# A hybrid attention layer on one core: the compressed branch on four partition groups, and five events moved in the order of the work

## Chip, core and metric

The kernel runs on one core of a Trainium2 chip. The metric is the device time in microseconds (us). The kernel before took 374.5 us in the median of three runs (374.48 to 375.17). All data is float32; matmuls marked fp32r take their operands in the faster reduced form of float32.

## What is computed

One decoder layer for 256 tokens of width 1024, cut to what matters here:

```python
h = rmsnorm(x, norm1_g)
proj = h @ w_in            # NSA q | NSA k, v (3 branches) | gates | MoBA q, k, v | merge gates
kc = compress(k_c, pe_k, w1_k, w2_k)   # 15 overlapping blocks of 32 tokens:
vc = compress(v_c, pe_v, w1_v, w2_v)   #   gelu(block @ w1) @ w2
y_A = g0 * attn(q, kc, vc) + g1 * attn(q_rot, k_s, v_s) + g2 * attn(q_rot, k_w, v_w)
y_B = attn(qm_rot, km_rot, vm)         # MoBA; 256 tokens are one block
x += (sig(gA) * (y_A @ w_up_nsa) + sig(gB) * (y_B @ w_up_moba)) @ w_out
x += relu(rmsnorm(x, norm2_g) @ w_ff1) ** 2 @ w_ff2
return rmsnorm(x, norm_f_g)
```

The NSA part has 8 query heads on 2 key groups, the MoBA part 8 heads; a head has 64 columns. The compressed branch is `attn(q, kc, vc)` with the two `compress` calls: 15 compressed keys for each of the 2 groups, so 30 columns.

## The kernel before, in words

**Large products.** Each large float32 product is made of three fp32r matmuls (`mm3`, line 237): high part by high part, high by low, low by high. For this each weight chunk (1 MB, 128 x 2048) is loaded, ScalarE (ACT) rounds it to a high part (`whi`, line 114), and VectorE (DVE) subtracts to get the low part (`wlo`, line 116). There are three buffers each for raw chunks, high and low parts.

**Slots.** The work is a row of slots, one for each of the 60 weight chunks c (`CHUNKS`, line 24; the last two share one): 0 and 1 keys and values `kva`, 2 and 3 `kvb`, 4 and 5 NSA queries `q`, 6 and 7 MoBA queries `qm`, 8 and 9 `km`, 10 and 11 `vm`, 12 to 19 the merge gates, 20 to 23 the two up-projections `upn` and `upm`, 24 to 27 `wout`, from 28 on the feed-forward layer. A slot is a list of matmuls (24 in the projections), and `run_slot` (line 220) issues them in order on TensorE (PE). Everything else is an event: `at(0.45, f, ...)` puts the call f ahead of the first matmul at or beyond 0.45 of the slot's list, and all that f issues goes in that order to the queue of each engine. Events with equal positions keep the order in which they were noted. So the positions are an order written out by hand, and each engine takes its instructions strictly in that order. `split_events` (line 272) places the high parts, low parts and the next load of chunk c + 2; `std_events` picks their positions.

**Compressed branch.** `cmp_gather` and `gather_evac` (slot 3) put the keys and values of the 15 blocks into `kE`, for l = 0 to 15 a tile of 128 rows (two tokens by 64) and 30 columns. `cmp_mlp1` (slot 4, line 381) multiplies with the first weights: 32 matmuls with 64 weight columns, keys into partitions 0 to 63, values into 64 to 127, 30 columns moving; behind it stands the GELU chain on ACT and DVE. `cmp_mlp2` (slot 5, line 393) applies the second weights and spreads the results into block-diagonal `bdk` (for the scores) and `bdv` (for the values). `cmp_scores` (slot 7, line 416) makes the scores of 8 heads in 8 matmuls, each with 128 query rows as weights and the 30 columns of `bdk` moving, and runs the softmax on the same tile. `cmp_probs_t` (slot 8, line 438) transposes the probabilities in 8 pieces of 30 columns into `pcT`. `d_trans` (line 518) later multiplies `bdv` and `pcT` into the output of each NSA head pair.

**Window, selected and MoBA attention.** Units d = 0 to 5 (`unit_events`, line 563) do two heads in two branches, or four MoBA heads, in the odd slots from 9: scores (`d_scores`), row maxima on DVE (`d_max`), eight exponentials on ACT (`d_exp`), then normalising, transposing and multiplying with the values (`d_pv`).

**PSUM banks.** The projections alternate between two banks (`acc0`, `acc1`; `tp` joins at the gates), and `tp` and `yb` serve the small work. A bank is free again when ACT or DVE has evicted it; `evac_tm` (line 296) evicts a projection's half.

**Feed-forward.** A round is one `ff1` chunk (48 matmuls of 256 columns) and one `ff2` chunk. The first 13 `ff2` chunks use seven products instead of eight (`seven_mms`, line 929), each into its own bank; the last of the seven, "4", is issued in two halves of 256 columns (`mm3_halves`, line 242) from the second round on, and whole in the first. `combine` (line 941) later adds the seven banks in three steps. `act_parts` makes the high and low parts (`ah`, `al`) of the activations.

Of the kernel before, what the change touches and what calls it, by code (L numbers as in the profile page):

```python
# [17 lines left out]
NCMP = 15  # L18
# [27 lines left out]
def hybrid_layer(ctx: ExitStack, tc: tile.TileContext, gxd, w, w1c, small, const, gf, out):  # L46
# [79 lines left out]
    pcT = ap_.tile([128, 4, 256], F32, name="pcT")  # L126
    bdv = ap_.tile([128, 128], F32, name="bdv")
# [27 lines left out]
    pool.memset(pcT, 0.0)  # L155
    pool.memset(bdv, 0.0)
# [85 lines left out]
    def mm3_halves(o, lh, ll, rh, rl, first, last):  # L242

        return [m for x in (slice(0, 256), slice(256, 512))
                for m in mm3(o[:, x], lh, ll, rh[:, x], rl[:, x], first, last)]
# [35 lines left out]
    def std_events(c):  # L281
        if 9 <= c < 20 and c % 2:
            split_events(c, (0.0, 0.06), (0.09, 0.46))
        elif 9 <= c < 20:
            split_events(c, (0.0, 0.45), (0.3, 0.8))
        else:
            split_events(c, (0.0, 0.45), (0.3, 0.46))
# [64 lines left out]
    kE = ap_.tile([128, 2, 16, 30], F32, name="kE")  # L352
    bdk = ap_.tile([128, 30], F32, name="bdk")
# [14 lines left out]
    def gather_evac(s):  # L368
        tp = U["kc", s]
        for l2 in range(2):  # L370
            p0 = l2 * 64
            v = tp[p0:p0 + 64].rearrange("p (g i l m) -> p g l i m", g=2, l=8, m=2)
            for lh in range(2):
                ls = slice(lh * 8, (lh + 1) * 8)
                o = kE[p0:p0 + 64, s, ls, :].rearrange("p l (g i) -> p g l i", g=2)
# [17 lines left out]
    def cmp_mlp2():  # L393
        tk = tp_tile()
        mm(tk[:, 0:30], w2[0:64, :], gl[0:64, 3, :], True, True)
        tv = tk[:, 128:256]
        mm(tv[0:30, 0:128], gl[64:128, 3, :], w2[64:128, :], True, True)
        dve.tensor_tensor(bdk, tk[:, 0:30], kc_[:, K_BDK:K_BDK + 30], op=ALU.mult)
        dve.tensor_tensor(bdv[0:30, :], tv[0:30, 0:128], kc_[0:30, K_BDV:K_BDV + 128],
                          op=ALU.mult)  # L400

    def gate_evac():
        for t in range(2):
# [8 lines left out]
    pcs = (ap_.tile([128, 256], F32, name="pcs")[:, 0:240]  # L412
           .rearrange("p (q t h i) -> p q t h i", q=4, t=2, h=2))
    st4 = ap_.tile([128, 112], F32, name="st4")[:, 0:64].rearrange("p (a b) -> p a b", a=4)

    def cmp_scores():
        tp = tp_tile()
        for p in range(4):
            for t in range(2):
                o = (p * 2 + t) * 30  # L420
                mm(tp[:, o:o + 30], qT[:, p, t * 128:(t + 1) * 128], bdk, True, True)
        s4 = tp[:, 0:240].rearrange("p (q t h i) -> p q t h i", q=4, t=2, h=2)
        for t in range(2):
            dve.tensor_tensor(pcs[:, :, t], s4[:, :, t],
                              cmpm[:, t, None, None, :].to_broadcast([128, 4, 2, NCMP]), op=ALU.add)
        s = pcs.rearrange("p q t h i -> p (q t h) i")
        dve.tensor_reduce(st4[:, 0], s, op=ALU.max, axis=AX)
        dve.tensor_scalar(st4[:, 0], st4[:, 0], -1.0e30, None, op0=ALU.max)
        dve.tensor_tensor(s, s, st4[:, 0, :, None].to_broadcast([128, 16, NCMP]), op=ALU.subtract)
# [4 lines left out]
        dve.tensor_tensor(st4[:, 3], st4[:, 2], gates[:, 0].rearrange("p q t h -> p (q t h)"),  # L434
                          op=ALU.mult)
        dve.tensor_tensor(s, s, st4[:, 3, :, None].to_broadcast([128, 16, NCMP]), op=ALU.mult)

    def cmp_probs_t():
        for i in range(2):
            tp = tp_tile()  # L440
            for j in range(2):
                for t in range(2):
                    o = j * 256 + t * 128
                    pe.transpose(tp[0:30, o:o + 128],
                                 pcs[:, 2 * i + j, t].rearrange("p h i -> p (h i)"), ident)
            act.activation(pcT[0:30, 2 * i:2 * i + 2, :].rearrange("p a q -> p (a q)"),
                           tp[0:30, :], AF.Copy)
# [70 lines left out]
    def d_trans(d):  # L518
# [19 lines left out]
        if kind == "n":  # L538
            mm(U["y"][:, p % 2], bdv, pcT[:, p, :], True, False)
# [45 lines left out]
    for sec, c0, n in groups:  # L585
# [6 lines left out]
        for i in range(2):  # L592
# [598 lines left out]
```

## Time and profile before

| | us |
|---|---|
| median of three runs | 374.5 |
| lowest and highest run | 374.48, 375.17 |
| the profiled execution | 373.52 |
| its span, first to last instruction | 371.5 |
| PE, DVE, ACT, POOL busy | 363.2, 310.2, 234.7, 4.9 |

The granted clock of TensorE is 0.995 of full speed on the mean. In the timeline and the chain a row gives the start in us from the span's first instruction, the duration, the engine, the line, the operation with output and inputs, the shape (for a matmul weight rows times weight columns, then moving elements), how many instructions the row merges, and in brackets the idle time before it with what ended it. PEld is the loading of weights, which overlaps PE. A matmul's duration contains its way through the pipeline, so the next one starts long before it ends. "SPq" and the like are an engine's queue, which issues DMAs. Helpers such as `mm` (line 235) carry the line for all their callers, so rows are told apart by their tiles.

### The profile page before, as it was taken

The page shows a single profiled execution, that of the slowest core. Times are in us where ns is not written, and L with a number is a line of the kernel's source. Part 1 is how long each engine was busy: PE and PEld are TensorE (multiplying, and loading weights), DVE is VectorE, ACT ScalarE, POOL GpSimd, SP SyncE. Part 2 cuts the span into 40 slices and gives each one's busy share as a digit, 9 for nine tenths or more (in the row PEclk, how much of TensorE's full clock was granted, in tenths as well). Part 3 has the DMA queues.
Part 4 walks back from the last instruction along what each step waited for, and adds up shares of the span by engine and source line. Part 5 has one row for each costly group of instructions (what it writes and reads, how often), then busy time and mean ns, then how long its engine had stood idle before and what let it go on. Part 6 is the DMA issues. An engine that isn't in the chain of part 4 may idle for free.

```text
span 371.5 us, 5941 instructions
## 1 busy us (share of the span) xinstructions
PE 363.2 (98%) x2387; PEld 321.2 (86%) x2387; DVE 310.2 (84%) x449; ACT 234.7 (63%) x352; POOL 4.9 (1%) x13
## 2 busy tenths in 40 slices
PE   8999999999999999999999999999999999999993
PEld 7998888877778887778999999999999999999973
DVE  4897677896868769766877999999999999995875
ACT  5983455847747567525465897876666677764522
POOL 1020000000000000000000000000000000000000
PEclk9999999999999999999999999999999999999997
DMA  8986535333444333532483655454555656654003
GB/s 281 392 326 226 196 109 213 113 115 114 141 160 153 114 114 130 211 128 100 168 313 124 248 226 205 168 192 181 182 215 220 226 228 227 225 178 165 0 0 113
DMA packets 11402, 66.28 MB, mean 178 GB/s; under 512 B 1264, under 2 KB 3056, under 8 KB 4080
## 3 DMA queue, kind: packets, MB, share of 16 engines
q1 hardware_dynamic: 10512, 64.55, 47.1%
q10 hardware_dynamic: 864, 1.38, 1.1%
q8 instruction: 18, 0.29, 0.3%
q14 instruction: 8, 0.07, 0.1%
HBM read 64.87 MB, written 1.05 MB: 177 GB/s over the span
## 4 chain that ended last, share of the span: by engine, by line
PE 88%; DVE 4%; ACT 3%; DMA 2%; issue 2%; POOLq 0%; POOL 0%; DVEq 0%; ACTq 0%
PE acc L235 58%; PE o L235 10%; PE yb L235 5%; PE tp L235 4%; PE qacc L235 3%; PE kvbacc L235 2%; DMA raw<-in_kva_dram 2%; DVE wlo L116 2%; PE Sa L531 1%; PE Sa L235 1%; ACT whi L114 1%; PE tp L321 1%; PE Sb L531 1%; DVE ust L491 1%; ACT P L501 1%
## 5 line engine op out<-in xcount | busy, mean ns | idle before, releaser
L116 DVE TENSOR_TENSOR wlo<-raw,whi 128x1024 fp32r<-128x1024 f32 (+3 forms) x85 | 109.8, 1311 | 14.0 <-ACT whi L114 14.0
L114 ACT ACTIVATE whi<-raw 128x1024 fp32r<-128x1024 f32 (+3 forms) x84 | 93.3, 1138 | 29.8 <-PE acc L235 22.0
L235 PE MATMUL acc<-h2h,whi 128*128 128x256 f32 x256 | 71.0, 277 | 0.0
L235 PE MATMUL acc<-h2l,whi 128*128 128x256 f32 x256 | 70.8, 277 | 0.0
L235 PE MATMUL acc<-h2h,wlo 128*128 128x256 f32 x256 | 70.8, 276 | 0.0
L235 PE MATMUL acc<-whi,hTh 128*128 128x512 f32 (+1 forms) x128 | 50.9, 398 | 0.3 <-ACT vm L301 0.3
L235 PE MATMUL acc<-wlo,hTh 128*128 128x512 f32 (+1 forms) x128 | 50.7, 396 | 0.2 <-DVE wlo L116 0.2
L235 PE MATMUL acc<-whi,hTl 128*128 128x512 f32 (+1 forms) x128 | 49.4, 386 | 0.0
L235 PEld LDWEIGHTS acc<-h2l,whi 128*128 128x128 f32 x256 | 48.1, 188 | 0.0
L235 PEld LDWEIGHTS acc<-h2h,whi 128*128 128x128 f32 x256 | 48.1, 188 | 0.0
L235 PEld LDWEIGHTS acc<-h2h,wlo 128*128 128x128 f32 x256 | 48.1, 188 | 0.0
L920 ACT ACTIVATE whi<-wt 128x2048 fp32r<-128x2048 f32 x13 | 25.0, 1922 | 25.7 <-PE acc L235 24.6
L922 DVE TENSOR_TENSOR wlo<-wt,whi 128x2048 fp32r<-128x2048 f32 x13 | 29.8, 2292 | 0.1
L235 PEld LDWEIGHTS acc<-whi,hTh 128*128 128x128 f32 x128 | 24.3, 190 | 6.4 <-issue 0.9
L235 PEld LDWEIGHTS acc<-wlo,hTh 128*128 128x128 f32 x128 | 24.2, 189 | 4.8 <-DVE wlo L116 0.9
L235 PEld LDWEIGHTS acc<-whi,hTl 128*128 128x128 f32 x128 | 24.2, 189 | 4.5
L913 DVE TENSOR_TENSOR sl<-raw,sh 128x1536 fp32r<-128x1536 f32 x13 | 22.9, 1758 | 0.0
L911 ACT ACTIVATE sh<-raw 128x1536 fp32r<-128x1536 f32 x13 | 19.4, 1490 | 2.9 <-PE acc L235 2.9
L235 PE MATMUL acc<-mxl,whi 128*128 128x256 f32 x64 | 17.8, 278 | 0.0
L235 PE MATMUL acc<-mxh,wlo 128*128 128x256 f32 x64 | 17.8, 278 | 0.0
L235 PE MATMUL acc<-mxh,whi 128*128 128x256 f32 x64 | 17.7, 276 | 0.0
L870 ACT ACTIVATE ah<-aq 128x896 fp32r<-128x896 f32 (+1 forms) x16 | 14.1, 880 | 3.9 <-PE acc L235 2.2
(270 smaller groups left out, 739.5 us busy)
## 6 DMA issues: line engine op xcount, KB each, us to landing
raw<-in_ff_dram SPq DMA_DIRECT2D x32, 1024.0 KB, 5.2
raw<-in_gm_dram SPq DMA_DIRECT2D x8, 1024.0 KB, 4.8
raw<-in_wout_dram SPq DMA_DIRECT2D x4, 1024.0 KB, 4.8
raw<-in_q_dram SPq DMA_DIRECT2D x2, 1024.0 KB, 5.1
raw<-in_qm_dram SPq DMA_DIRECT2D x2, 1024.0 KB, 6.6
raw<-in_km_dram SPq DMA_DIRECT2D x2, 1024.0 KB, 4.9
raw<-in_vm_dram SPq DMA_DIRECT2D x2, 1024.0 KB, 4.8
raw<-in_upn_dram SPq DMA_DIRECT2D x2, 1024.0 KB, 5.7
```

Source lines behind the costliest of these rows:

```text
L114: act.activation(hi[c][:, a:b], raw[c][:, a:b], AF.Copy)
L116: dve.tensor_tensor(lo[c][:, a:b], raw[c][:, a:b], hi[c][:, a:b].bitcast(F32), op=ALU.subtract)
L235: pe.matmul(o, l, r, start=start, stop=stop, skip_group_check=True)
L321: pe.transpose(tp[:, j * 256 + t * 128:j * 256 + t * 128 + 128], src[:, t, (2 * i + j) * 128:(2 * i + j + 1) * 128], ident)
L491: dve.tensor_reduce(o, S, op=ALU.max, axis=AX)
L501: act.activation(P[:, 2 * x + j, a:b], S[:, j, x], AF.Exp, scale=0.125, bias=st[:, 1, i:i + 1], accum_out=st[:, 2, i:i + 1])
L531: pe.transpose(T[:, j, x, o:o + 128], P[:, 2 * x + j, c:c + 128], ident)
L870: act.activation(A[i][1][:, 0:b - a], aq[:, a:b], AF.Copy)
L911: act.activation(singles[c][0], v, AF.Copy)
L913: dve.tensor_tensor(singles[c][1], v, singles[c][0].bitcast(F32), op=ALU.subtract)
L920: act.activation(hi[c], v, AF.Copy)
L922: dve.tensor_tensor(lo[c], v, hi[c].bitcast(F32), op=ALU.subtract)
```

## The change

- **First compressed MLP.** Weights and moving operand are swapped: the 32 padded columns of `kE` are the weights, the 64 columns of `w1` move. Keys and values, each with even and odd l, go to four groups of 32 partitions. A new `cmp_sum` (slot 5, 0.09) adds even and odd with two matmuls against a 0/1 matrix `gsum`, which DVE makes from the identity; the GELU chain now stands behind it.
- **Second MLP.** The value product is made four times, into the four groups, and `bdv` becomes one block-diagonal matrix for each head pair.
- **Scores.** Four matmuls with `bdk` as weights (32 columns) and 256 query columns moving, one in each group, evicted by ACT into `kva`. A new `cmp_softmax` (0.25) transposes them back in two pieces and runs the same softmax. `cmp_probs_t` needs two transposes. The second transposes of the NSA queries move from 0.5 to 0.25.
- **Order of events.** Slot 7 (MoBA queries): the second high part moves from 0.45 to 0.51, behind an eviction at 0.5, the second low part from 0.46 to 0.52. Slot 11: the eviction of `vm` moves from 0.5 to 0.49, ahead of the exponentials, the first key transposes from 0.02 to 0.09. Slot 22 (`upm`): the second low part moves from 0.1 to 0.53, behind an eviction at 0.52, and the load with it. First of the last `ff2` slots: `combine` step 2 moves from 0.52 to 0.54, behind `act_parts`.
- **First round of `ff2`.** Product "4" is issued as one whole first matmul and then halves.
- Tiles change place in SBUF; those not named here keep their addresses.

The diff, cut to its core:

```diff
     def mm3_halves(o, lh, ll, rh, rl, first, last):
-        return [m for x in (slice(0, 256), slice(256, 512))
-                for m in mm3(o[:, x], lh, ll, rh[:, x], rl[:, x], first, last)]
+        r = mm3(o, lh, ll, rh, rl, first, last)[:int(first)]
+        return r + [m for x in (slice(0, 256), slice(256, 512))
+                    for m in mm3(o[:, x], lh, ll, rh[:, x], rl[:, x], first, last)[int(first):]]
...
     def std_events(c):
-        if 9 <= c < 20 and c % 2:
+        if c == C_QM + 1:
+            split_events(c, (0.0, 0.51), (0.3, 0.52))
+        elif 9 <= c < 20 and c % 2:
...
         for l in range(16):
             for s in range(2):
-                mm(tp[s * 64:(s + 1) * 64, 0:30], w1[:, s, l, :], kE[:, s, l, :], l == 0, l == 15)
+                g = 64 * s + 32 * (l % 2)
+                mm(tp[g:g + 32, 0:64], kE[:, s, l, :], w1[:, s, l, :], l < 2, l >= 14)
+        act.activation(raw1, tp[:, 0:64], AF.Copy)
+        dve.tensor_reduce(gsum, ident.rearrange("p (g i) -> p i g", g=4), op=ALU.add, axis=AX)
+
+    def cmp_sum():
+        tp = tp_tile()
+        for s in range(2):
+            r = slice(s * 64, (s + 1) * 64)
+            mm(tp[r, 0:30], raw1[r, :], gsum[r, 0:30], True, True)
...
         mm(tk[:, 0:30], w2[0:64, :], gl[0:64, 3, :], True, True)
-        tv = tk[:, 128:256]
-        mm(tv[0:30, 0:128], gl[64:128, 3, :], w2[64:128, :], True, True)
+        groups = [slice(g * 32, g * 32 + 30) for g in range(4)]
+        for r in groups:
+            mm(tk[r, 128:256], gl[64:128, 3, :], w2[64:128, :], True, True)
...
     def cmp_scores():
-        tp = tp_tile()
+        tp = ps_e.tile([128, 512], F32, name="kvbacc0")
         for p in range(4):
-            for t in range(2):
-                o = (p * 2 + t) * 30
-                mm(tp[:, o:o + 30], qT[:, p, t * 128:(t + 1) * 128], bdk, True, True)
+            mm(tp[32 * p:32 * p + 32, 0:256], bdk, qT[:, p, :], True, True)
+        act.activation(kva.rearrange("p t d -> p (t d)"), tp[:, 0:256], AF.Copy)
+
+    def cmp_softmax():
+        tp = ps_e.tile([128, 512], F32, name="kvbacc1")
+        for t in range(2):
+            pe.transpose(tp[:, t * 128:(t + 1) * 128], kva[:, t, :], ident)
...
     def cmp_probs_t():
-        for i in range(2):
-            tp = tp_tile()
-            for j in range(2):
-                for t in range(2):
-                    o = j * 256 + t * 128
-                    pe.transpose(tp[0:30, o:o + 128],
-                                 pcs[:, 2 * i + j, t].rearrange("p h i -> p (h i)"), ident)
+        tp = tp_tile()
+        for t in range(2):
+            pe.transpose(tp[:, t * 128:(t + 1) * 128],
+                         pcs[:, t].rearrange("p q x -> p (q x)"), ident)
...
-            mm(U["y"][:, p % 2], bdv, pcT[:, p, :], True, False)
+            mm(U["y"][:, p % 2], bdv[:, p, :], pcT, True, False)
...
+                at(0.09, cmp_sum)
...
-                at(0.5, transp_heads, tm["q"], qrT, 0, 1)
+                at(0.25, cmp_softmax)
+                at(0.25, transp_heads, tm["q"], qrT, 0, 1)
...
-                at(0.02, transp_heads, tm["km"], kmT, 0)
+                at(0.09, transp_heads, tm["km"], kmT, 0)
...
-                at(0.5, evac_tm, sec, 0, accs[0], n)
+                at(0.49 if sec == "vm" else 0.5, evac_tm, sec, 0, accs[0], n)
...
-            elif c < C_UPM + 1:
+            elif c == C_UPM:
+                split_events(c, (0.0, 0.0), (0.1, 0.53))
+            elif c < C_UPM:
                 split_events(c, (0.0, 0.0), (0.1, 0.1))
...
-            f = mm3_halves if name == SEVEN[-1][0] and i else mm3
+            f = mm3_halves if name == SEVEN[-1][0] else mm3
...
-                at(0.52, combine, 2)
+                at(0.54, combine, 2)
```

More of the change, by code (lines that the diff above doesn't have):

```diff
@@ L125, in hybrid_layer @@
     kc_ = cp.tile([128, K_N], F32, name="kc")
-    pcT = ap_.tile([128, 4, 256], F32, name="pcT")
-    bdv = ap_.tile([128, 128], F32, name="bdv")
+    kE = ap_.tile([128, 2, 16, 32], F32, name="kE")
+    raw1 = ap_.tile([128, 64], F32, name="raw1")
+    gsum = ap_.tile([128, 32], F32, name="gsum")
+    bdk = ap_.tile([128, 32], F32, name="bdk")
     w1 = ap_.tile([128, 2, 16, 64], F32, name="w1", tag="w1")
@@ L154, in hybrid_layer @@
     pool.memset(ones, 1.0)
-    pool.memset(pcT, 0.0)
-    pool.memset(bdv, 0.0)
+    pool.memset(kE[:, :, :, 30:32], 0.0)
+    pool.memset(bdk[:, 30:32], 0.0)
     xT = gx[:, 16:].rearrange("p (k q) -> p k q", k=8)
@@ L349, in transp_k @@
         split_evac(tp[:, None, 0:256], dst)
-    kE = ap_.tile([128, 2, 16, 30], F32, name="kE")
-    bdk = ap_.tile([128, 30], F32, name="bdk")
+    bdv = ap_.tile([128, 4, 128], F32, name="bdv")
+    pcT = ap_.tile([128, 256], F32, name="pcT")
+    ap_.tile([128, 224], F32, name="gap4")
+    pool.memset(bdv, 0.0)
     gl = ap_.tile([128, 4, 30], F32, name="gl")
@@ L374, in gather_evac @@
                 ls = slice(lh * 8, (lh + 1) * 8)
-                o = kE[p0:p0 + 64, s, ls, :].rearrange("p l (g i) -> p g l i", g=2)
+                o = kE[p0:p0 + 64, s, ls, 0:30].rearrange("p l (g i) -> p g l i", g=2)
                 dve.tensor_tensor(
@@ L395, in cmp_mlp2 @@
         mm(tk[:, 0:30], w2[0:64, :], gl[0:64, 3, :], True, True)
-        tv = tk[:, 128:256]
-        mm(tv[0:30, 0:128], gl[64:128, 3, :], w2[64:128, :], True, True)
-        dve.tensor_tensor(bdk, tk[:, 0:30], kc_[:, K_BDK:K_BDK + 30], op=ALU.mult)
-        dve.tensor_tensor(bdv[0:30, :], tv[0:30, 0:128], kc_[0:30, K_BDV:K_BDV + 128],
-                          op=ALU.mult)
+        groups = [slice(g * 32, g * 32 + 30) for g in range(4)]
+        for r in groups:
+            mm(tk[r, 128:256], gl[64:128, 3, :], w2[64:128, :], True, True)
+        dve.tensor_tensor(bdk[:, 0:30], tk[:, 0:30], kc_[:, K_BDK:K_BDK + 30], op=ALU.mult)
+        for g, r in enumerate(groups):
+            dve.tensor_tensor(bdv[r, g, :], tk[r, 128:256], kc_[r, K_BDV:K_BDV + 128],
+                              op=ALU.mult)
     def gate_evac():
@@ L433, in cmp_scores @@
         dve.reciprocal(st4[:, 2], st4[:, 1])
-        dve.tensor_tensor(st4[:, 3], st4[:, 2], gates[:, 0].rearrange("p q t h -> p (q t h)"),
-                          op=ALU.mult)
-        dve.tensor_tensor(s, s, st4[:, 3, :, None].to_broadcast([128, 16, NCMP]), op=ALU.mult)
+        for t in range(2):
+            b = slice(4 * t, 4 * t + 4)
+            dve.tensor_tensor(st4[:, 3, b], st4[:, 2, b], gates[:, 0, :, t, :], op=ALU.mult)
+        dve.tensor_tensor(s, s, each(3), op=ALU.mult)
     def cmp_probs_t():
-        for i in range(2):
-            tp = tp_tile()
-            for j in range(2):
-                for t in range(2):
-                    o = j * 256 + t * 128
-                    pe.transpose(tp[0:30, o:o + 128],
-                                 pcs[:, 2 * i + j, t].rearrange("p h i -> p (h i)"), ident)
-            act.activation(pcT[0:30, 2 * i:2 * i + 2, :].rearrange("p a q -> p (a q)"),
-                           tp[0:30, :], AF.Copy)
+        tp = tp_tile()
+        for t in range(2):
+            pe.transpose(tp[:, t * 128:(t + 1) * 128],
+                         pcs[:, t].rearrange("p q x -> p (q x)"), ident)
+        act.activation(pcT, tp[:, 0:256], AF.Copy)
     yTh = {m: ap_.tile([128, 4, 256], F32R, name=f"yTh{m}") for m in "nm"}
@@ L1165, in _layout @@
     con[:, K_BDK:K_BDK + 30] = 0.5 * (r[:, None] // 64 == np.arange(30)[None, :] // 15)
-    con[:30, K_BDV:K_BDV + 128] = 0.5 * (np.arange(30)[:, None] // 15 == r[None, :] // 64)
+    con[:, K_BDV:K_BDV + 128] = 0.5 * (r[:, None] % 32 // 15 == r[None, :] // 64)
     return ({k: c(v) for k, v in d.items()}, c(w1), c(small), con,
```

19 lines of the change are left out of this document (12 added, 7 removed).

## The prediction, made before the change was run

> **What bounds the kernel now.** I read the page first: the busy line, then the chain that ended last.
>
> ```profile
> span 371.5 us, 5941 instructions
> ...
> PE 363.2 (98%) x2387; PEld 321.2 (86%) x2387; DVE 310.2 (84%) x449; ACT 234.7 (63%) x352; POOL 4.9 (1%) x13
> ...
> PE 88%; DVE 4%; ACT 3%; DMA 2%; issue 2%; POOLq 0%; POOL 0%; DVEq 0%; ACTq 0%
> ```
>
> TensorE is busy for 98% of the span and carries 88% of the chain. So a change pays where it takes time out of TensorE's stream, or ends one of the few waits of that stream. The waits of PE alone, which I read next, name them (left out: one at the very start, and shorter ones):
>
> ```profile
> PE acc L235 <- ACT vm L301: 0.3, 1, 0.3
> PE yb L717 <- DVE sga L710: 0.3, 1, 0.3
> PE tp L235 <- DVE al L872: 0.2, 1, 0.2
> ```
>
> These are the three places where the change moves an eviction ahead of exponentials, an eviction ahead of a low part, and a low part ahead of a combine. Since busy rows overlap (a matmul's row is longer than its share of the stream), I measure everything below from start to start in the timeline.
>
> One thing could undo this: VectorE in the feed-forward stage.
>
> ```profile
> 240.00:260.00 20.00, 20.00 (x142) 18.57 (x142) 20.00 (x23) 14.25 (x12) 0.00 (x0) 1.00 0.54 203
> ```
>
> Columns are PE, PEld, DVE, ACT and POOL, then the granted clock (1.00). VectorE is as full as TensorE there. But among PE's waits only the one on `al` lies in that stage, near its end; TensorE leads, and what comes earlier shifts the whole stage earlier.
>
> **The compressed branch, part by part.** First the rates that I need.
>
> ```profile
> 28.06 0.39 PE L235 MATMUL qacc<-whi,hTh 128*128 128x512 f32 x1
> 28.29 0.39 PE L235 MATMUL qacc<-wlo,hTh 128*128 128x512 f32 x1
> 28.61 2.06 PE L235 MATMUL tp<-kE,w 128*64 128x30 f32 x64
> 30.59 0.50 PE L235 MATMUL qacc<-whi,hTl 128*128 128x512 f32 x1
> ```
>
> ```profile
> 77.69 1.52 PE L235 MATMUL yb<-PT,kvb 128*64 128x256 f32 x16
> 79.14 0.50 PE L235 MATMUL acc<-whi,hTh 128*128 128x512 f32 x1
> ```
>
> ```profile
> L235 PE MATMUL yb<-PT,kvb x16: 272/326/430, 77.7 to 78.9; 128*64 128x256 f32 x8, 128*64 128x128 f32 x8
> ```
>
> ```profile
> 55.78 0.87 PE tp L444 x8
> ```
>
> ```profile
> 73.80 0.43 PE yb L235 x2
> ```
>
> A large matmul has 0.23 us to itself (28.06 to 28.29). A full fp32 matmul appears as two instructions (32 calls in the first MLP, x64). Eight transposes of 128 columns take 0.87, so 0.109 each; two instructions of 256 columns take 0.43, so 0.218 each: time goes with the moving columns. The 16 instructions of a probabilities-times-values step would thus take 8 x 0.218 + 8 x 0.109 = 2.62 us one by one, yet the next matmul starts 1.45 us later (77.69 to 79.14): the two halves of 64 columns run together (1.31), and 0.14 is the way out of that mode. The way in costs 28.29 to 28.61 less 0.23, so 0.09.
>
> *First MLP product (`cmp_mlp1`).* Its 64 instructions take 1.98 us (28.61 to 30.59), 31 ns each, in pairs: 32 steps of some 58 ns and 0.12 at the end. With 30 moving columns the step is set by the 64 weight columns. The change swaps the operands: weights of 32 columns, 64 moving columns, four groups. A step of 64 columns is half of a transpose's 0.109, with the same few ns on top 58 ns; 16 steps of four are 0.93 + 0.12 = 1.05. Gain 0.93, if four groups run together. No row here shows four groups: the bounds are a gain of 0.93 and a loss of 1.85 (64 steps of 58 ns, 3.71 + 0.12, one after the other). I take the gain, since the nearest rows show groups of columns running side by side in full.
>
> On this step the Trainium skill has a rule against the change. "TensorE: Matmul & The Clock Gate", in the section on the gap of 56 ns, says that start-to-start of matmuls never falls below about 25 ns however few columns move; by it 64 instructions take an estimated 1.60 us and the gain would be 0.38. The 31 ns here neither break nor prove it.
>
> *The added sum (`cmp_sum`) and the second MLP.*
>
> ```profile
> 36.42 0.39 PE L235 MATMUL qacc<-whi,hTl 128*128 128x512 f32 x1
> 36.74 0.40 PE L235 MATMUL tp<-gl,sm 64*128 64x30 f32 x2
> 37.07 0.40 PE L235 MATMUL tp<-sm,gl 64*30 64x128 f32 x2
> 37.40 0.44 PE L348 MATMUL tp<-ident,kvb 128*128 128x128 f32 x2
> ```
>
> The two small products of the second MLP take 0.33 each, with a change of mode in each. The sum adds two products on opposite quarters of the array, two instructions each: one such piece, 0.33, plus the way in, 0.09, is 0.42 (bounds 0.33 and 0.75, both pieces and the way in). The value product becomes four, one in each group of 32, 128 columns moving: 0.05 together, 0.66 more if one by one.
>
> Around it ACT gets one eviction, DVE one small reduction and three more multiplies. Their cover, from the timelines of ACT and of DVE:
>
> ```profile
> 30.71 0.20 ACT L386 ACTIVATE gl<-tp 128x30 f32<-128x30 f32 x1 [3.37 <-PE tp L235]
> ```
>
> ```profile
> 31.86 0.19 DVE L391 SCALAR_TENSOR_TENSOR gl<-gl 128x30 f32<-128x30 f32 x1 [0.30 <-ACT gl L390]
> ```
>
> ACT had idled 3.37 us before the old eviction, and DVE waited for that eviction in turn; the new eviction and the reduction go there. The GELU chain, 30.71 to 32.05 or 1.34 us, now starts behind the sum. The sum stands at 0.09 of the next slot and the chain's reader at 0.75; at 24 matmuls of 0.23 a slot that is 3.6 us for 1.34. Behind it on both queues wait the split of the window keys and one weight split, moved by about a microsecond and needed later still. I cost all this at nothing; without its cover it would be 1.34.
>
> *Scores, softmax, transposes back.*
>
> ```profile
> 46.12 1.86 PE L235 MATMUL tp<-bdk,qT 128*128 128x30 f32 x16
> 47.82 0.48 PE L235 MATMUL acc<-whi,hTh 128*128 128x512 f32 x1
> ```
>
> Sixteen instructions take 1.70 us, set by 128 weight columns each. The new four matmuls move 256 columns in four groups: 2 x 0.218 + 0.14 + 0.09 = 0.67 together (1.97 one by one). Gain 1.03. Two transposes bring the scores back: 2 x 0.109 = 0.22 more. The probabilities need two transposes for eight: 6 x 0.109 = 0.65 less.
>
> The change adds a wait: the transposes need ACT's eviction of the scores.
>
> ```profile
> 37.88 0.39 ACT L339 ACTIVATE kswh<-tp 128x256 fp32r<-128x256 f32 x1 [1.70 <-PE tp L348]
> ```
>
> ```profile
> 45.69 1.06 ACT L114 ACTIVATE whi<-raw 128x1024 fp32r<-128x1024 f32 x1 [2.87 <-PE acc L235]
> ```
>
> An eviction of that size is 0.39. Scores issue from 46.2; their second half starts 0.22 later and is out some 0.4 after that (instructions of 256 columns last up to 0.43 in the rows above), about 46.8, when the split of 45.69 has just left ACT (46.75). The eviction ends near 47.25. TensorE has the scores' 2 x 0.218 + 0.14 and three large matmuls in hand: 46.2 + 0.58 + 3 x 0.23 = 47.47. So it fits by about 0.2: cost nothing, rival below. Behind the transposes the query transposes move earlier; the ACT high part (position 0.45 to 0.51) now stands behind the eviction of the MoBA queries, with two slots until it is read: nothing either way.
>
> **First product in pieces.**
>
> ```profile
> 218.94 0.68 PE tp L235 x3
> 219.62 5.65 PE acc L235 x48
> ...
> 229.35 0.71 PE tp L235 x6
> 230.06 5.46 PE acc L235 x48
> ```
>
> In the first round the last product is three matmuls of 512 columns, and the 48 behind it take 5.65 us, 118 ns each. In the next round it is in halves: 0.03 more, and the 48 take 5.46. The change gives the first round the second's form (one whole, four halves): gain 0.16.
>
> **The three waits.**
>
> ```profile
> 84.31 0.39 PE L235 MATMUL acc<-whi,hTl 128*128 128x512 f32 x1
> 85.02 0.50 PE L235 MATMUL acc<-whi,hTh 128*128 128x512 f32 x1 [0.32 <-ACT vm L301]
> ```
>
> ```profile
> 162.85 2.36 DVE L116 TENSOR_TENSOR wlo<-raw,whi 128x1024 fp32r<-128x1024 f32 x2 [0.46 <-ACT whi L114]
> ```
>
> ```profile
> 166.04 0.39 PE L235 MATMUL acc<-whi,yTlm 128*128 128x512 f32 x1
> 166.69 0.63 PE L717 MATMUL yb<-ident,sga 128*128 128x128 f32 x4 [0.26 <-DVE sga L710]
> ```
>
> ```profile
> 355.33 0.39 PE L235 MATMUL tp<-wlo,ah 128*128 128x512 f32 x1
> 355.93 0.50 PE L235 MATMUL tp<-whi,al 128*128 128x512 f32 x1 [0.21 <-DVE al L872]
> ```
>
> Start to start less 0.23 each: 85.02 - 84.31 gives 0.48, 166.69 - 166.04 gives 0.42, 355.93 - 355.33 gives 0.37; 1.27 in all. At 85 the eviction that frees the bank stands behind four exponentials; put ahead of them it ends sooner by about as much as those four take, and the last of all eight exponentials ends when it did, because today the eviction stands in their middle. At 166 one of the two low parts (half of 2.36) goes behind the upsampling evictions, 1.18 against a wait of 0.42; its reader is the output stage, two slots on, and the load that follows it on SP's queue moves by half a slot, three slots ahead of its use. At 355 the `al` subtraction goes ahead of two combine steps; what waits for those is the final stage. Next late in each place is TensorE itself. The MoBA key transposes (0.02 to 0.09) let a weight split pass; nothing.
>
> **Sum.** 0.93 - 0.42 - 0.05 + 1.03 - 0.22 + 0.65 + 0.16 = 2.08 on TensorE's stream, and 1.27 of waits: 3.35. The profiled execution, 373.52 us (span 371.5 and 2.0 around it), becomes 370.17. It lies 0.98 under the median of 374.5; against the median the forecast is 371.15, so 371.1.
>
> **Rivals.** (1) *Only two groups at a time.* The rows show two, never four. The first MLP then gains nothing (0.93), scores lose 0.44, the value product 0.22: 371.15 + 1.59 = 372.7. For it: no row shows more; against: nothing saturates at two. (2) *An issue floor.* If 31 ns an instruction is what the stream can do, the first MLP alone gains nothing: 372.1; the scores, with few and long instructions, keep their gain. The page cited above would put its floor a little lower. (3) *The groups run one after another, and the kernel is slower.* Place: the three four-group steps. Price: 2.78 in the first MLP (a loss of 1.85 for a gain of 0.93), 1.30 in the scores, 0.66 in the value product: 371.15 + 4.74 = 375.9. It decides once these steps lose 3.35 against my sum. Against it stands the 1.45 us where 2.62 would be serial. (4) *The scores' eviction comes late* behind a split of 1.06 that started late: 1.06 less the room of 0.2 is 0.86 of TensorE idle, 372.0. (5) *The waits only move* to another engine's late step, though the mechanism works on TensorE: 1.27 back, 372.4.
>
> **How the numbers follow.** Forecast 0.50; rival 1 0.17; 2 0.13; 3 0.05; 4 0.08; 5 0.07. The range runs from 370.1 (the sum against the profiled execution itself, 370.17) to 372.9, which takes in rivals 1, 2, 4 and 5; outside are rival 3 and two rivals at once. About 0.2% (0.75 us) is what a measurement of this kernel can tell from no change. Faster 0.92: all cases but rival 3 and a sum of rivals 1, 5 and a piece of 4 (same, 0.03); slower 0.05.
>
> **What would show it.** Right: the first MLP's 64 instructions within 1.1 us, the scores' eight within 0.7, two transposes behind them with no wait on ACT, 5.46 in place of 5.65, and no wait of PE on `vm`, `sga` or `al`. Wrong: the first MLP near 2 us (rivals 1 or 2; the scores at 0.65 or 1.1 tell which) or near 3.8 (rival 3); a PE wait on `kva` near 47; DVE rows in PE's waits after 200.

## The result and the profile after

The changed kernel took 371.43 us in the median of six runs (370.43 to 372.15), the kernel before beside it 374.49 (374.34 to 375.17): ratio 0.9914, 95% interval 0.9897 to 0.9931. So it is faster by 3.06 us where 3.35 were forecast. The profiled execution took 371.17 us.

The page of the changed kernel, its lines for the span, the busy engines and the chain that ended last:

```profile
span 369.4 us, 5952 instructions
...
PE 360.8 (98%) x2387; PEld 318.5 (86%) x2387; DVE 311.6 (84%) x454; ACT 234.2 (63%) x353; POOL 3.7 (1%) x15
...
PE 93%; DMA 1%; ACT 1%; issue 1%; DVE 1%; SPq 0%; POOLq 0%; POOL 0%; DVEq 0%
```

TensorE has the same number of instructions and is busy 2.4 us less; VectorE's share of the chain fell from 4% to 1%, because the waits that ended on it are gone. All waits of PE that the trace names:

```profile
PE yb L156 <- POOL ones L157: 1.3, 1, 1.3
PE tp L372 <- ACT kcd L304: 0.5, 1, 0.5
PE acc L238 <- ACT whi L114: 0.3, 1, 0.3
```

`vm`, `sga` and `al` are no longer there. The second line is at 23.5 us, where the change moved nothing; e3_again below tells what it is. The third is at 8.0 us, among the first products of all; seven of the kernels below have one there too, of 0.2 to 0.6. The timeline of PE through the compressed branch (columns as before; lines moved by 3, `mm` is now line 238):

```profile
29.50 0.39 PE L238 MATMUL qacc<-wlo,hTh 128*128 128x512 f32 x1
29.82 1.10 PE L238 MATMUL tp<-w,kE 128*32 128x64 f32 x64
30.85 0.50 PE L238 MATMUL qacc<-whi,hTl 128*128 128x512 f32 x1
...
33.02 0.39 PE L238 MATMUL qacc<-whi,hTl 128*128 128x512 f32 x1
33.34 0.30 PE L238 MATMUL tp<-gsum,raw 64*64 64x30 f32 x4
33.57 0.44 PE L354 MATMUL tp<-ident,kva 128*128 128x128 f32 x2
...
46.84 0.64 PE L238 MATMUL kvbacc<-qT,bdk 128*32 128x256 f32 x8
47.41 0.50 PE L238 MATMUL acc<-whi,hTh 128*128 128x512 f32 x1
47.74 0.39 PE L238 MATMUL acc<-wlo,hTh 128*128 128x512 f32 x1
47.97 0.40 PE L238 MATMUL acc<-whi,hTl 128*128 128x512 f32 x1
48.21 0.38 PE L445 MATMUL kvbacc<-ident,kva 128*128 128x128 f32 x2
```

The first MLP product takes 1.03 us from its start to the next product's (29.82 to 30.85), the scores 0.57 (46.84 to 47.41). Their eviction is ready for the transposes at 48.21, as ACT's timeline shows:

```profile
46.31 1.06 ACT L114 ACTIVATE whi<-raw 128x1024 fp32r<-128x1024 f32 x1 [2.85 <-PE acc L238]
47.54 0.39 ACT L440 ACTIVATE kva<-kvbacc 128x256 f32<-128x256 f32 x1 [0.17 <-PE kvbacc L238]
```

The eviction ends at 47.93, 0.28 ahead of the transposes; the split had left ACT in time. The chain's row of the `ff1` products behind the first `ff2` round, once 5.65:

```profile
218.02 5.46 PE acc L238 x48
```

And the `sga` transposes, which had waited for VectorE, now start in step with the products ahead of them (0.23):

```profile
164.88 0.39 PE L238 MATMUL acc<-whi,yTlm 128*128 128x512 f32 x1
165.11 0.60 PE L744 MATMUL yb<-ident,sga 128*128 128x128 f32 x4
```

To set kernels side by side, this table cuts the span of each at the start of the first product of a kind on PE: first q product (slot 4), first attention score (slot 9), first `upn`, `wout` and `ff1` product, last `ff1` product, last product, end. All in us, one profiled execution each.

| kernel | to q | q to score | to upn | to wout | to ff1 | to last ff1 | to last product | to end | span |
|---|---|---|---|---|---|---|---|---|---|
| before | 24.64 | 36.07 | 86.91 | 26.16 | 22.82 | 151.59 | 16.99 | 6.31 | 371.5 |
| after | 25.85 | 34.04 | 86.52 | 25.75 | 22.82 | 151.43 | 16.48 | 6.50 | 369.4 |
| e1_branch | 24.34 | 34.02 | 86.93 | 26.17 | 23.60 | 151.90 | 17.00 | 6.49 | 370.5 |
| e2_order | 25.12 | 36.06 | 86.46 | 25.75 | 22.82 | 151.43 | 16.48 | 6.32 | 370.4 |
| e3_again | 24.61 | 34.03 | 86.54 | 25.75 | 23.60 | 151.74 | 16.48 | 6.49 | 369.2 |
| e4_two_groups | 25.21 | 34.72 | 86.53 | 25.75 | 22.82 | 151.43 | 16.48 | 6.49 | 369.4 |
| e5_place11 | 24.64 | 34.03 | 86.28 | 25.71 | 23.52 | 152.04 | 16.48 | 6.49 | 369.2 |
| e6_place9 | 24.92 | 34.02 | 86.29 | 25.71 | 23.72 | 152.04 | 16.48 | 6.49 | 369.7 |
| e7_start | 24.99 | 34.21 | 86.53 | 25.75 | 23.60 | 151.74 | 16.48 | 6.59 | 369.9 |
| e9_cols | 25.41 | 33.74 | 86.44 | 25.71 | 22.82 | 151.43 | 16.48 | 6.50 | 368.5 |
| e10_nudge | 24.62 | 34.05 | 86.25 | 25.71 | 24.86 | 151.43 | 16.48 | 6.50 | 369.9 |
| e11_pieces | 25.15 | 34.04 | 86.26 | 25.71 | 23.58 | 151.43 | 16.48 | 6.50 | 369.1 |
| e12_one_piece | 25.21 | 34.06 | 86.26 | 25.71 | 22.94 | 151.43 | 16.48 | 6.50 | 368.6 |
| e13_piece_late | 24.24 | 34.04 | 86.25 | 25.71 | 22.83 | 151.43 | 16.48 | 6.49 | 367.5 |

From before to after the stages behind the first q product give 2.03 + 0.39 + 0.41 + 0.00 + 0.16 + 0.51 - 0.19 = 3.31. The profiled spans differ by only 2.10, because in this execution the stretch up to the first q product was 1.21 longer. In the columns to ff1 and to last ff1 five kernels (e1_branch, e3_again, e5_place11, e6_place9, e7_start) have some 0.8 and 0.3 to 0.6 more than their edits account for; that is one of two rhythms of the same products, told further down.

### The profile page after: what moved, and what is told of

Read it like the earlier page. It is cut to its first block, busy times and chain, and to the rows that moved or that the text cites. A ratio compares the mean times of both kernels' runs of the same rounds, so it can differ in the third digit from the quotient of the medians.

```text
span 369.4 us, 5952 instructions
## 1 busy us (share of the span) xinstructions
PE 360.8 (98%) x2387; PEld 318.5 (86%) x2387; DVE 311.6 (84%) x454; ACT 234.2 (63%) x353; POOL 3.7 (1%) x15
## 3 DMA queue, kind: packets, MB, share of 16 engines
HBM read 64.87 MB, written 1.05 MB: 178 GB/s over the span
## 4 chain that ended last, share of the span: by engine, by line
PE 93%; DMA 1%; ACT 1%; issue 1%; DVE 1%; SPq 0%; POOLq 0%; POOL 0%; DVEq 0%
PE acc L238 62%; PE o L238 10%; PE yb L238 6%; PE tp L238 4%; PE qacc L238 3%; PE kvbacc L238 2%; PE Sa L238 2%; PE Sa L556 1%; DMA gx<-in_gx_dram 1%; PE tp L327 1%; PE Sb L556 1%; ACT whi L114 1%; PE Sb L238 1%; PE o L843 0%; DVE wlo L116 0%
## 5 line engine op out<-in xcount | busy, mean ns | idle before, releaser
L901 DVE TENSOR_TENSOR al<-aq,ah 128x896 fp32r<-128x896 f32 (+1 forms) x16 | 16.2, 1011 | 0.6 <-ACT ah L899 0.6
```

The costliest lines, as they stand in the source:

```text
L901: dve.tensor_tensor(A[i][2][:, 0:b - a], aq[:, a:b], A[i][1][:, 0:b - a].bitcast(F32), op=ALU.subtract)
```

## Experiments

**The two halves of the change, the change again, and two groups.** The first kernel keeps the compressed branch and puts the order of events and the first round's product back; the second is the rest of the change alone; the third is the changed kernel once more.

```diff
# e1_branch, against after
-        if c == C_QM + 1:
-            split_events(c, (0.0, 0.51), (0.3, 0.52))
-        elif 9 <= c < 20 and c % 2:
+        if 9 <= c < 20 and c % 2:
...
-                at(0.49 if sec == "vm" else 0.5, evac_tm, sec, 0, accs[0], n)
+                at(0.5, evac_tm, sec, 0, accs[0], n)
...
-            f = mm3_halves if name == SEVEN[-1][0] else mm3
+            f = mm3_halves if name == SEVEN[-1][0] and i else mm3
...
# (and upm's low part, the key transposes and combine step 2; e2_order: the change's side of these places alone, against before)
```

> The compressed branch on four groups alone; the moved events and the first product in pieces are as before. Theory (TensorE's stream is the bound, four groups run together): 2.0 us under the kernel before, since the steps measured in the profile after add up to 0.95 - 0.30 - 0.05 + 1.04 - 0.28 + 0.65; the waits of PE on vm, sga and al come back at their old size (0.48, 0.42, 0.37 from start to start). Rival (the branch's gain shows only where the waits are gone): the waits grow by what the stream gains, and the run is within 0.7 us of the kernel before. On the start: if it is the branch that delays the start (new memsets, other places in SBUF), the first q product is 1.2 us later than in the kernel before, as in the profile after; if that is chance, it can lie anywhere between.

> The moved events and the first product in pieces alone; the compressed branch is as before. Theory (independent parts): 1.5 us under the kernel before, 0.60 at vm, 0.41 at sga, 0.48 less some of it at al, 0.17 in the first round, 0.18 given back to a new wait on P near 88. Rival (the waits only move): under 0.7 us. On the start: this kernel has the memsets and places of the kernel before, so its first q product should stand where it stood there if the branch is what delays the start.

> The changed kernel once more, on the chip of the other three. Theory: 3.1 to 3.5 us under the kernel before, and the place of the first q product (26.0 in the profile after, 24.8 in the one before) is chance of the first loads, so it differs from the first profile by some tenths or more. Rival (the change delays its own start): it stands at 26.0 again, within 0.2.

Measured: e1_branch 372.74 us (ratio to before 0.9955, 0.9939 to 0.9971), e2_order 372.32 (0.994, 0.9917 to 0.9963), e3_again 370.3 (0.9894, 0.9868 to 0.9921). Both halves are faster than before by themselves. Beside a kernel before of 374.23 the medians are 1.49, 1.91 and 3.93 lower, where 2.0, 1.5 and 3.1 to 3.5 were expected: medians miss by half a microsecond here, so the sizes are read by stage. The table shows that they don't touch each other: the branch is worth 2.05 between the first q product and the first score, in e1_branch as in the whole change, and nothing behind it but the tail (its two larger columns around `ff1` are the rhythm just named); the order's gains stand in the later columns of e2_order. The waits of PE in e1_branch:

```profile
PE acc L238 <- ACT vm L305: 0.3, 1, 0.3
PE yb L742 <- DVE sga L735: 0.3, 1, 0.3
PE tp L238 <- DVE al L897: 0.2, 1, 0.2
```

They are the three of before, word for word but for the lines: the branch moved its 2 us earlier and every wait came along. Putting the events back is what brings them back, so the moves are what had removed them. The moves were put back together, not one by one: that each wait went by the move at its own place is read from the places, and the two moves that were forecast at nothing (the high part in slot 7, the key transposes) have no test of their own.

e3_again also answers for the long start of the first profile. ACT's timeline of after, and then that of e3_again, the same program:

```profile
20.07 2.01 ACT L114 ACTIVATE whi<-raw 128x1024 fp32r<-128x1024 f32 x2 [2.21 <-DVE wlo L116]
21.98 0.67 ACT L304 ACTIVATE kcd<-acc,rstd 128x512 f32<-128x512 f32 x1
```

```profile
17.71 2.00 ACT L114 ACTIVATE whi<-raw 128x1024 fp32r<-128x1024 f32 x2 [0.26 <-DVE xsq L207]
20.23 0.69 ACT L304 ACTIVATE kcd<-acc,rstd 128x512 f32<-128x512 f32 x1 [0.51 <-POOL rstd L214]
```

In after ACT stood idle for 2.21 us ahead of the high part of chunk 4. The row names VectorE, but the rows of that chunk's load, issued at 12.9 and 12.5 us, tell it (time from issue to landing at the end), again of after and of e3_again:

```profile
raw<-in_q_dram SPq DMA_DIRECT2D x1, 1024.0 KB, 7.1
```

```profile
raw<-in_q_dram SPq DMA_DIRECT2D x1, 1024.0 KB, 5.1
```

12.9 + 7.1 is 20.0, where the high part starts. The eviction `kcd` waited behind it, and PE for that (0.5 in the waits above). In e3_again the load is there by 17.6 and nothing of this happens; its first q product comes at 24.61. Of the 1.24 between the two, 0.83 lies behind the first kvb product and is this load (11.10 and 10.27 us from there to the first q product); the other 0.41 was there already when that product started (14.76 and 14.35), ahead of any use of chunk 4. Over all kernels of the table the first q product comes between 24.24 and 25.85, with no link to the edit to be seen.

But e3_again differs in a second place: 23.60 instead of 22.82 before `ff1`, with the same instructions. That was not expected; the later experiments follow it.

The fourth kernel keeps the swapped operands and lets only two groups work at a time: even l first, then odd.

```diff
-        for l in range(16):
+        for l in sorted(range(16), key=lambda l: l % 2):
```

> The changed kernel with the first MLP's 32 matmuls in another order, all even l and then all odd l, so that neighbours use only two of the four groups of 32 columns; the same instructions and the same sums. Theory (the gain comes from four groups running together, a step lasts as long as 64 columns move): 32 steps of 56 to 58 ns, so the first MLP takes 1.9 to 2.0 us instead of 1.03, and the kernel is 0.9 us slower than the changed one. Rival (what counts is the instruction, 16 ns each, or the 32 weight columns): 1.0 to 1.1 us, no difference.

```profile
29.17 1.79 PE L238 MATMUL tp<-w,kE 128*32 128x64 f32 x64
30.90 0.50 PE L238 MATMUL qacc<-whi,hTl 128*128 128x512 f32 x1
```

The same 64 instructions take 1.73 us, and the stage is 0.68 longer than in after; the median is 370.5 (0.9908, 0.9882 to 0.9934), so 0.7 us don't stand out in whole runs here, while the trace shows them. By the starts of the single instructions a pair takes 56 ns, where before had 58. The row is 0.2 us shorter than the 1.9 expected because of its middle, where the even l end and the odd begin and all four groups are in use: seven pairs take 0.20 us there instead of 0.39. In after a set of four takes 56 ns (16 sets, and 0.13 for the way out): the second pair runs inside the time of the first. The gain is the groups', not that of the swapped operands.

**What sets a step.** Half of the 64 columns of the first MLP product move. The kernel leaves out the other half of the hidden units, so it doesn't compute the layer, and only its trace is read (one execution).

```diff
-                mm(tp[g:g + 32, 0:64], kE[:, s, l, :], w1[:, s, l, :], l < 2, l >= 14)
+                mm(tp[g:g + 32, 0:32], kE[:, s, l, :], w1[:, s, l, 0:32], l < 2, l >= 14)
...
# (the eviction into raw1 writes these 32 columns twice)
```

> Changed kernel, but the first MLP product of the compressed branch moves 32 of its 64 columns: half of the hidden units are left out (the other half stands in their place), so the time alone is read. Four groups of 64 columns take 1.03 us, 56 ns for each step of four products with two instructions each... 64 products, 16 ns each. Theory of the prediction (a step lasts as long as the columns that move): 32 columns take 25 to 30 ns a step, 0.5 to 0.6 us in all, first q product to first score 34.05 -> 33.6. Rival (16 ns is what a product costs whatever it moves): 1.03 us, 34.05.

```profile
29.38 0.76 PE L238 MATMUL tp<-w,kE 128*32 128x32 f32 x64
30.07 0.50 PE L238 MATMUL qacc<-whi,hTl 128*128 128x512 f32 x1
```

0.69 us, and 0.30 less to the first score. In the first half of the row, where the sets are regular, a set of four takes 32 or 33 ns instead of 56; the second half has uneven steps. So 64 moving columns set the step of 56, and 16 ns was no cost of an instruction. It isn't in full proportion: half the columns would be 28, and with the 0.13 for the way out 0.58 us; the gain is two thirds of that expected. What holds the step above 28, the 32 weight columns or a cost of each instruction, was not tested.

**A wait that the change made, and the late start.** With `vm` evicted first, the exponentials of slot 11 end at the same time as before the change, counted from the first score, while PE arrives earlier. Rows of before, VectorE's normalising of `P` and PE's transposes of it, with 0.52 us of room between them (88.94 to 89.46):

```profile
87.11 1.83 DVE L515 TENSOR_TENSOR P<-P,ust 128x512 f32<-128x512 f32 x2
```

```profile
89.46 1.03 PE L531 MATMUL Sa<-ident,P 128*128 128x128 f32 x8
```

The same of after:

```profile
86.27 1.83 DVE L540 TENSOR_TENSOR P<-P,ust 128x512 f32<-128x512 f32 x2
```

```profile
87.77 0.39 PE L238 MATMUL acc<-whi,hTh 128*128 128x512 f32 x1
88.15 0.66 PE L556 MATMUL Sa<-ident,P 128*128 128x128 f32 x4
```

The transposes start 0.38 after the product ahead instead of 0.23, when VectorE is done (88.10). The next kernels move four of the exponentials ahead of a key eviction that nobody needs soon; two of them also move the last transposes of the mix, for the second matter below.

```diff
-            at(0.2 if s > 12 else 0.5, d_exp, d, 1)
+            at(0.2 if s > 12 else 0.3 if s == 11 else 0.5, d_exp, d, 1)
...
-            at(0.2, lambda: mix_t(1, 1, s_tile(1)[:, 0]))
+            at(0.21, lambda: mix_t(1, 1, s_tile(1)[:, 0]))    # e6_place9: 0.18
...
```

> Changed kernel with two moves. (a) In the first output-projection slot the last transposes of the mix, mix_t(1, 1), go one product later (before product 11 of 48 instead of 10). (b) In slot 11 the exponentials of the rows t=1 of the second unit stand ahead of the second eviction of the MoBA keys (0.3 instead of 0.5). In the six traces so far the stretch from the first output-projection product to the first feed-forward product takes 22.82 us (four) or 23.60 (two), at 113 or 118 ns per 256-column product, and the pace is fixed within five products after these transposes: where TensorE came back from its short wait for sga with a step of 172 ns the pace was 113, with 170 it was 118. Theory (the coming back from a wait draws the pace): one product later sga is there, no wait, so the pace is 113: 22.8 us, and the six times lie closer together, none above 371.5. Rival (the pace is drawn by something else): 23.6 us in about one trace of three, spread as before (369.5 to 372.3). For (b): the wait of the first transposes of P at 88.15, 0.15 to 0.18 us, goes: first score to first upn product 86.51 -> 86.33; rival, the later eviction of vm makes TensorE wait again: 86.8 or more. Time by the theories: 370.0; by the rivals 371.0.

> As e5_place11, but mix_t(1, 1) goes one product earlier (before product 9), a place between two triples of products, and with the same move of the exponentials. Theory (the coming back from a wait draws the pace): TensorE waits longer for sga, by about 0.1 us, and comes back at a moment that ScalarE's or VectorE's end sets, so the pace is still drawn: 22.8 or 23.6 us, either is possible. Rival (the place within the triple of products decides): always one pace in this kernel. One trace alone can't tell these two apart; the spread of the six times helps: under 1 us for the rival, up to 2 us by the theory.

In e5_place11 VectorE's row starts at 83.93 and PE's timeline has no gap:

```profile
86.56 0.39 PE L238 MATMUL acc<-whi,hTh 128*128 128x512 f32 x1
86.80 0.60 PE L556 MATMUL Sa<-ident,P 128*128 128x128 f32 x4
```

The stage to `upn` is 86.28, 0.24 to 0.26 less than in after and e3_again, and 86.25 to 86.29 in all six kernels with this move. So the new wait had cost 0.25, where 0.15 to 0.18 were expected. Medians: e5_place11 369.89 (0.9878, 0.9855 to 0.9901), e6_place9 371.25 (0.9908, 0.9883 to 0.9932).

For the start, the evictions of `kva` went ahead of the high parts:

```diff
-                for k in range(2):
-                    at(0.0, split, 4, k, 2, "h")
                 for t in range(2):
-                    at(0.01, evac_tm, "kva", t, first[t], 384)
+                    at(0.0, evac_tm, "kva", t, first[t], 384)
+                for k in range(2):
+                    at(0.01, split, 4, k, 2, "h")
```

> Changed kernel with one move: in slot 3 the evictions of kva (kcd and kva, 1.8 us on ScalarE) stand ahead of the high parts of chunk 4 instead of behind them. In the changed kernel's first profiled run these high parts waited until 20.07 for their load, the evictions behind them, and TensorE's kcd transposes 0.73 us for these; in its second run the load was there by 17.7 and TensorE waited for nothing. Theory: the wait is one of order on ScalarE, so now the transposes never wait for it, and from the first kvb product to the first q product it is 10.26 us in every run; with late loads 0.4 to 0.7 us less than 11.09, with early ones nothing, so a median of 370.1 to 370.6. Rival: the high parts and with them the low parts of chunk 4 come late (the evictions end at 21.5, high parts 23.5, low parts 24.8), and the q products wait: 0.3 to 0.8 us more in every run, 371.

```profile
20.60 0.69 ACT L304 ACTIVATE kcd<-acc,rstd 128x512 f32<-128x512 f32 x1 [2.79 <-POOL rstd L214]
```

The evictions now wait for nothing but `rstd`, and from the first kvb product to the first q product it is 10.28 us. But 10.27 or 10.28 is also what nine other traces show without the edit, and the next stage lost 0.17 (34.21), so it brought nothing here: 371.11 (0.9912, 0.9884 to 0.994) instead of 370.1 to 370.6. Whether it helps when the load is late was not seen; why the load is late in some runs stays open.

**Two rhythms of the same products.** The chain's row for the stretch from the last mix transposes to the x1 transposes, in e3_again and then in after:

```profile
173.25 29.92 PE acc L238 x254
```

```profile
174.49 28.82 PE acc L238 x254
```

The same 254 products of 256 columns take 118 ns each in one execution and 113 in the other, 1.10 us apart. In the slow one every third weight load lasts 192 ns instead of 188, and which of the three products it belongs to differs between kernels; the granted clock is 1.00 in both. The rhythm is settled within five products of the transposes; the last products ahead of them come at 113 or 114 in all fourteen traces. My first idea was that coming back from the short wait for `sga` draws it: in the eight traces with the transposes in the change's place and a step of 171 to 173 ns to the first of them it was 113, in the three with 169 or 170 it was 118. e5_place11, where that wait is gone, should then always have 113. It had 118 (23.52 for the stage), so this idea fell, and e13_piece_late, with the same place, had 113. The link between step and rhythm in those eleven traces stays without an explanation. That their place decides is out too: after and e3_again are the same program. Ahead of any added product the count over the fourteen traces is nine with 113 and five with 118. Two kernels, which keep the move of the exponentials, then interrupted the stream six times, by a product of two columns or by issuing one product in two pieces of 128:

```diff
+        if i:
+            for pos in (0.25, 0.75):
+                at(pos, lambda: mm(FB["n"][0:2, 0:2], ones, ones, True, True))    # e10_nudge
+                at(pos, piece.append, 1)    # e11_pieces: the next product in two pieces
...
```

> Changed kernel with the exponentials of e5_place11 moved, mix_t(1, 1) where the change has it, and six added products of 2 columns (into a bank that nothing reads), two in each of the last three output-projection slots, ahead of product 12 and of product 36: each interrupts the stream of 256-column products for a moment. Theory (113 and 118 ns a product are two steady rhythms of the same stream, and whatever interrupts it draws one of them anew): after some of the six the rhythm differs from the one ahead of it, in both directions or from 118 to 113 alone; the six cost 0.2 to 0.5 us themselves. Rival (the rhythm is a state of the chip that lasts through a run): the rhythm is the same ahead of and behind all six, and 22.8 + 0.4 or 23.6 + 0.4 us for the stage. The wait for P is gone (86.3 from first score to first upn product).

> As e10_nudge, but instead of an added product the product at the same six places is issued as two of 128 columns. Theory (the rhythm is drawn anew at each interruption): as there. A second one (products in pieces leave the stream at 113, as at the end of each feed-forward group in the change): 118 turns into 113 at the first piece and stays there, so the stage takes at most 22.9 us and what the six pieces cost, 0.1 to 0.5 us. Rival (a state of the chip): no change of rhythm at any of the six.

Medians 371.92 (0.9918, 0.9895 to 0.9941) and 370.51 (0.9879, 0.9857 to 0.99). All twelve interruptions began and ended at 113. The chain of e11_pieces has the same pattern at each:

```profile
179.18 0.17 PE acc L243 x2
179.35 2.68 PE acc L245 x23
182.02 0.17 PE acc L243 x2
182.19 2.68 PE acc L245 x23
```

A piece costs (23.58 - 22.82) / 6 = 0.13 us, a product of two columns (24.86 - 22.82) / 6 = 0.34. For all six that is 0.76 and 2.04, both more than expected (0.1 to 0.5, and 0.2 to 0.5). So 113 holds through these interruptions; 118 met none of them. It did meet the 16 transposes of x1, and there it went both ways. The 72 `ff1` products behind them, in e3_again and then in e5_place11, which both had come at 118:

```profile
204.91 8.17 PE acc L238 x72
```

```profile
204.56 8.48 PE acc L238 x72
```

That is 113 and 118: e1_branch, e3_again and e7_start came out at 113, e5_place11 and e6_place9 stayed at 118. So neither does an interruption always end the slow rhythm, nor must the rhythm last through a run. The last two kernels have one piece only, some seven products behind the mix transposes, in the change's place and one product later:

```diff
+            at(0.35, piece.append, 1)
```

> Changed kernel with the exponentials of e5_place11 moved, mix_t(1, 1) where the change has it, and one product in two pieces of 128 columns, product 16 or 17 of 48 in the first output-projection slot, some seven products behind the transposes. In the nine traces of kernels without added products the stage had 113 ns a product in five and 118 in four, in e5_place11 and e6_place9 too; each of the twelve interruptions of e10_nudge and e11_pieces began and ended at 113, and a piece cost 0.13 us. Theory (a piece leads to 113 from either rhythm): whatever the seven products ahead of it show, 113 behind it, stage 22.9 to 23.0 us, and 370.0 in the median with no time above 371.3. Rival (each rhythm keeps itself through an interruption): where the seven products show 118, it stays, 23.7 us.

> As e12_one_piece, with mix_t(1, 1) one product later as in e5_place11, where the rhythm behind it was 118. Theory: 118 for the few products ahead of the piece, 113 behind it, stage 22.85 to 23.0 us instead of 23.52, 370.0. Rival (each rhythm keeps itself): 118 behind it too, 23.6 us, 370.7.

(The expectation's "five and four" should read five and five, with e5_place11 and e6_place9 counted.) Both had 113 ahead of the piece already and kept it: stages of 22.94 and 22.83, medians 370.22 (0.9886, 0.9865 to 0.9907) and 370.07 (0.9887, 0.9865 to 0.9908). The question they were made for, whether a piece turns 118 into 113, stays open. Of the kernels that compute the whole layer they have the shortest profiled spans, 368.6 and 367.5 (the second with the earliest first q product of all), and hold the sure gain of 0.25 on `P`; but their ratios overlap those of the changed kernel (0.9914 and 0.9894), so whole runs don't show them to be faster than it.

## Why the prediction was right

The mechanism was the one forecast, four groups at once and three waits gone, and the size was 3.06 in the medians, or 3.31 by stages, for 3.35. That the sum came out within 0.04 is in part luck: the branch gave 0.11 more than its terms, the waits and the first round together 0.04 more, and 0.19 that nobody had counted was lost at the end. By its own steps:

- **First MLP** 1.05 forecast, 1.03 measured; the old 1.98 minus this is 0.95 for 0.93. A set of 64 columns takes 56 ns, forecast 58. Rivals 1 and 3 are out: two groups alone need 1.73, and the scores would have shown it too. Rival 2, an issue floor, is out: 64 instructions in 1.03 us are 16 ns each, in e9_cols 11. By this the rule of the Trainium skill ("TensorE: Matmul & The Clock Gate", the section on the gap of 56 ns: never below about 25 ns from start to start) does not hold across column groups, where this trace has starts of neighbours 6 to 7 ns apart. The measurement decides. The trace of before could have told it: its 31 ns an instruction are a mean, of 6 or 7 ns from the first of a pair to the second and some 52 to the next pair.
- **The sum** cost 0.32 (33.02 to 33.57 is 0.55, less 0.23 for the product ahead), forecast 0.42. The term was taken from one small product of the second MLP, with a change of mode on either side; here two pieces stand between the same two changes, 0.23 from the start of the first to the transposes. The GELU chain behind the sum cost nothing, as forecast: PE has no wait there.
- **Scores** 0.57 and 0.09 for the way in, 0.66 for 0.67. The eviction was in time by 0.28, forecast 0.2 (rival 4 out). The branch as a whole gave 2.03 where these terms sum to 1.92.
- **Halves** 151.59 to 151.43, 0.16 as forecast.
- **The waits.** This is the step that was mis-sized, twice and in opposite directions. The waits gave more: `al` 0.51 for 0.37, `vm` some 0.60 for 0.48, `sga` 0.41 for 0.42. The prediction stopped at the start of the product that had waited; but such a product has a row of 0.50 instead of 0.39 and the one behind it starts 0.11 later. At `sga` transposes follow anyway, so nothing is added there. And "next late in each place is TensorE itself" was wrong at `vm`: next late was VectorE's normalising of `P`, 0.25. It was in the rows of before: exponentials in the same total, an end that doesn't move, and a PE that comes 0.6 sooner where there is 0.52 of room. 1.52 less 0.25 is 1.27 (the columns of the table give 1.31), the forecast's own number, by chance. Rival 5 was true of this one wait in part.
- **What it didn't count**: 0.18 behind the last product (6.31 to 6.49), in every kernel with the new branch and in neither without it; the last instructions up to the issue of the output's DMA are alike, so it lies in or behind the transfer. Its cause wasn't sought.

The range of 370.1 to 372.9 held all six runs; of the six of e3_again, the same program, two lay below it (369.53 and 369.68). What moved single executions most was none of its rivals: the loads at the start (1.2 us to the first q product, 0.8 of it by chunk 4) and the rhythm around the output stage (1.1 us) are both of the size of the run-to-run spread. That they make it up is likely but not shown, since only profiled executions have a trace.

## What to carry to other kernels

Small products that use 32 of TensorE's columns run four at a time if each writes its own group of 32 partitions and they are issued in turn; with 64 moving columns a set of four then costs what a pair does, with 32 somewhat more than half of that. Turn the operands so that the short side is the weights. When a wait of the full engine goes, price it to the second product behind it, and then ask of every other engine on the path whether its end moved too: here one of three removed waits gave back 0.25 at the next reader. Compare kernels by stage in the trace before comparing medians: 0.25 and 0.7 us were plain there and lost among runs that spread over 2 us.

## What the hardware showed beside this

- Four column groups take neighbouring instructions 6 to 7 ns apart, and a set of four costs what a pair on two groups does: 56 ns with 64 float32 columns (e4_two_groups has 56 a pair); with 32 columns it is 32 ns.
- A stream of 256-column fp32r products keeps one of two rhythms, 113 or 118 ns, over 250 products with nothing in the program to tell them apart. Only the period is clear: in the slow one, one load in three takes 4 ns longer. At the transposes of x1 the slow one ended in three of five executions and went on in two.
- The change's "pieces" of the first round met the same pair: 5.65 for 48 products is 118 ns, 5.46 is 114.
- A 128-column piece of an fp32r product starts 57 ns after its twin, half of the 113 of the whole; of the 0.13 us that a split costs, 57 ns come behind the second piece (113 ns to the next start, for 128 columns) and 57 behind the product after it (170 for 113), the rest in the next three.
